# Query, key and value products of two chunks at a time by seven block products, with the query norm applied in the attention's sigmoid

## The chip, the cores and the metric

One core of a Trainium2 chip runs the whole program. The metric is device time in microseconds (us), the median of the runs shown. All arrays are float32. For TensorE the program keeps each operand as a pair of tiles of type float32r, a rounded high part and the rest (low part), and a product is three matmuls: high by high, low by high, high by low.

## What is computed

Two layers over 2048 tokens of 1024 channels. Layer A is a gated pooling mixer; layer B is causal stick-breaking attention with 16 heads of 64. What matters here, cut from the reference:

```python
kv_in = rms_norm(x, kv_norm)
k_all, v_all = jnp.split(kv_in @ w_kv, 2, axis=-1)
k_sh = rms_norm(split_heads(k_all), k_norm)
v_sh = split_heads(v_all)
h = rms_norm(x, b_norm[j])
q, z = jnp.split(h @ b_w_in[j], 2, axis=-1)
q = rms_norm(split_heads(q), b_q_norm[j])
o = stick_breaking_attention(q, k_sh, v_sh)   # beta = sigmoid(q.k / sqrt(d))
```

q, k and v are each a product of the stream (2048 x 1024) with a 1024 x 1024 matrix, whose rows carry the norm's gain.

## The kernel before

The first part of the program walks over four chunks of 512 tokens. For each chunk, layer A runs as 16 steps: eight of `run_z` and `run_u` (input projection), four of `run_o` (output projection), four of `run_g` (gated embedding), each 48 to 60 matmuls of 128x512. Then come six steps of `run_kvq` (L530 on): q, k, v, two column halves each. A step takes its weights as pairs from a list of loads made one step ahead (`load_w`: SP starts the transfer, ScalarE scales by the gain at L112, VectorE takes the rest at L113; without a gain ScalarE casts at L106 and POOL or VectorE subtracts at L108). In `run_kvq` two banks take 48 matmuls in turns, 24 each (L536), with the chunk's tokens as rows of the bank. ScalarE empties a bank with the token's norm as scale (L617 for q and k, L579 for v). For q and k follow a square (L619), a sum over each head (L621), the root on POOL (L80), a multiplication on VectorE (L629), four transposes (L638) and a split (L646, L647 or L215, L216), then a store of 512 KB to `qd` or `kd` (L649). Values are shifted by a token with transfers of ScalarE's queue, subtracted on POOL (L609), cast (L610) and split (L611), then stored.

Beside the steps run pieces of other work: `prep` turns the next chunk's x into pairs (L266, L269, L270) inside `run_kvq`, and `keep` (L700 on, its stores at L713) splits weights that the attention will read back, one or two a step from step 8 of a chunk on.

The second part is the attention over all heads and chunks, one slot for 128 queries by 512 keys: two matmuls (L816, L817), a sigmoid of the negative logits on ScalarE (L820), a scan on VectorE (L825, L828), transposes (L841), a cast and a rest (L844, L845), two matmuls with the values (L853, L854), with the remaining projections in the gaps.

The order on each engine is made by a scheduler from the order of the code, priorities and its own estimate of costs; each engine then works through its list in order and waits by semaphores. The banks of the first part are six (`psd` four, `psboth` two) for products and two (`pst`) for transposes. Pools: `io` 10 tiles for transfers (shared), `wraw` 3, `act` 18 pairs, `tmp` 8, `wpair` 6 and 6.

## Time and profile before

| what | value |
|---|---|
| runs | 2768.14, 2768.68, 2774.12 us; median 2768.68 |
| profiled execution, from the first to the last instruction | 2765.4 us; its time outside the span isn't given apart, and the median lies 3.3 us above the span |
| TensorE / VectorE / ScalarE / POOL busy | 2725.7 / 1956.0 / 1385.5 / 873.7 us |
| first part (layer A, q, k, v) | 0 to 1364.6 us |
| q, k, v stages of chunks 0 to 3 | 143.1, 143.0, 143.6, 139.2 us |
| attention | 1364.6 to 2765.4 us |
| moved by DMA | 573.21 MB, mean 207 GB/s |

An engine that is busy the whole span can only finish earlier by doing less; one with idle time costs nothing unless the busy one waits for it. So the rows to read are TensorE's waits and the busy time of every engine stage by stage. A group's row gives the line, engine, operation, tiles written and read, the count, then busy us and mean ns of one, then idle time just before and what ended it. PE is TensorE, DVE is VectorE, ACT is ScalarE, POOL is GpSimd.

### The profile page before, as it was taken

How to read it: one execution, taken by the hardware profiler on the slowest of the kernel's cores; microseconds unless marked ns; L12 is line 12 of the kernel's file. 1: busy time of each engine (PE TensorE's matmuls, PEld its weight loads, DVE VectorE, ACT ScalarE, POOL GpSimd, SP SyncE). 2: the span in 40 equal slices, each digit the busy share in tenths (PEclk: the TensorE clock that was granted, in tenths of full speed). 3: DMA queues.
4: the chain of work that ended last, by engine and by line, in shares of the span. 5: the costliest groups of instructions: out<-in, count | busy, mean ns of one | idle time of the engine just before them, and what ended most of it. 6: DMA issues, size and time to landing. Idle time of an engine off the chain costs nothing. (4 is left out here: it accounts for less than half of the span.)

```text
span 2765.4 us, 39537 instructions
## 1 busy us (share of the span) xinstructions
PE 2725.7 (99%) x13715; PEld 2260.4 (82%) x13715; DVE 1956.0 (71%) x2573; ACT 1385.5 (50%) x2801; POOL 873.7 (32%) x695
## 2 busy tenths in 40 slices
PE   9999999999999999999999999999999999999999
PEld 7888888888888888888888888887887778888877
DVE  6766535655357544565499999999999988996632
ACT  5444532445234542345356566666666655664521
POOL 2574338642475325753121111111110011112220
PEclk9999999999999999999999999999999999999999
DMA  8664696747946479445678565555555566668765
GB/s 293 236 196 171 218 325 204 225 148 253 347 148 227 163 249 318 136 145 170 191 254 278 180 217 170 169 161 178 169 159 162 159 200 200 188 204 264 249 209 160
DMA packets 335835, 573.21 MB, mean 207 GB/s; under 512 B 32462, under 2 KB 166638, under 8 KB 335636
## 3 DMA queue, kind: packets, MB, share of 16 engines
q1 hardware_dynamic: 330186, 563.03, 63.5%
q10 hardware_dynamic: 5450, 7.66, 0.9%
q8 instruction: 108, 1.77, 0.3%
q14 instruction: 91, 0.75, 0.1%
HBM read 430.01 MB, written 132.19 MB: 203 GB/s over the span
## 5 line engine op out<-in xcount | busy, mean ns | idle before, releaser
L844 ACT CAST at<-psa 128x512 fp32r<-128x512 f32 (+3 forms) x640 | 334.1, 522 | 478.4 <-PE psa L841 459.6
L536 PE MATMUL psd<-wpair,x 128*128 128x512 f32 x2304 | 544.0, 393 | 0.0
L828 DVE TENSOR_TENSOR_SCAN pp<-kap,pp,zeros 128x512 f32<-128x512 f32 x384 | 512.9, 1336 | 3.1 <-ACT kap L820 2.4
L536 PEld LDWEIGHTS psd<-wpair,x 128*128 128x128 f32 x2304 | 428.2, 188 | 86.2
L845 DVE TENSOR_TENSOR at<-psa,at 128x512 fp32r<-128x512 f32 (+3 forms) x640 | 381.0, 596 | 88.0 <-ACT at L844 84.9
L841 PE MATMUL psa<-ident,pp 128*128 128x128 f32 x2176 | 347.0, 275 | 17.2 <-DVE at L845 15.5
L820 ACT ACTIVATE kap<-psl 128x512 f32<-128x512 f32 (+3 forms) x640 | 344.9, 539 | 15.1 <-PE psl L817 12.0
L841 PEld LDWEIGHTS psa<-ident,pp 128*128 128x128 f32 x2176 | 262.9, 140 | 93.0 <-DVE at L845 38.8
L816 PE MATMUL psl<-kk,qa 128*128 128x512 f32 (+3 forms) x640 | 281.4, 440 | 0.0
L854 PE MATMUL pso<-at,vv 128*128 128x512 f32 (+3 forms) x640 | 235.1, 367 | 0.0
L817 PE MATMUL psl<-kk,qb 128*128 128x512 f32 (+3 forms) x640 | 233.0, 364 | 0.0
L853 PE MATMUL pso<-at,vv 128*128 128x512 f32 (+3 forms) x640 | 232.7, 364 | 0.0
L825 DVE TENSOR_TENSOR_SCAN pp<-kap,ahead 128x128 f32<-128x128 f32 (+3 forms) x256 | 219.8, 859 | 5.8 <-ACT kap L820 4.1
L131 PE MATMUL psd<-xp,wpair 128*128 128x512 f32 x512 | 201.9, 395 | 1.3 <-ACT xp L269 0.8
L132 PE MATMUL psd<-xp,wpair 128*128 128x512 f32 x512 | 200.5, 392 | 0.0
L133 PE MATMUL psd<-xp,wpair 128*128 128x512 f32 x512 | 200.1, 391 | 0.0
L113 DVE SCALAR_TENSOR_TENSOR wpair<-wraw,gains,wpair 128x512 fp32r<-128x512 f32 x192 | 169.7, 905 | 36.8 <-ACT wpair L112 36.1
L923 POOL TENSOR_TENSOR zr<-zr,sgz 128x512 f32<-128x512 f32 x32 | 58.8, 1836 | 368.2 <-ACT sgz L922 311.3
L112 ACT ACTIVATE wpair<-wraw,gains 128x512 fp32r<-128x512 f32 x192 | 135.0, 720 | 59.0 <-PE psd L536 32.3
L108 POOL TENSOR_TENSOR wpair<-wraw,wpair 128x512 fp32r<-128x512 f32 x99 | 145.5, 1485 | 59.7 <-ACT wpair L106 59.7
L853 PEld LDWEIGHTS pso<-at,vv 128*128 128x128 f32 x640 | 120.2, 188 | 26.9 <-ACT at L844 0.2
L854 PEld LDWEIGHTS pso<-at,vv 128*128 128x128 f32 x640 | 120.3, 188 | 25.9
(211 smaller groups left out, 5402.4 us busy)
## 6 DMA issues: line engine op xcount, KB each, us to landing
kk<-kd SPq DMA_DIRECT2D x320, 128.0 KB
vv<-vd SPq DMA_DIRECT2D x160, 256.0 KB
wraw<-in_w_kv_dram SPq DMA_DIRECT2D x128, 256.0 KB
wpair<-wzd SPq DMA_DIRECT2D x64, 512.0 KB
wpair<-wod SPq DMA_DIRECT2D x64, 512.0 KB
wpair<-wgd SPq DMA_DIRECT2D x64, 512.0 KB
wpair<-wu SPq DMA_DIRECT2D x48, 512.0 KB
wpair<-wi SPq DMA_DIRECT2D x36, 512.0 KB
```

What stands on the lines that cost most here:

```text
L131: T.matmul(ps, wst(units, kt, 0, c0), acts[kt][:, 0], start=(begin and kt == order[0]), stop=False)
L536: T.matmul(pss2[i], ck["x2"][kt][:, xh, tk], wst(ws, kt, wh, 0, W5), start=(kt == 0 and xh == 0 and wh == 0), stop=(kt == KT - 1 and wh == 1))
L816: T.matmul(ps[:, :w], qa[:, qs], kk[:, :w], start=True, stop=False)
L817: T.matmul(ps[:, :w], qb[:, qs], kk[:, :w], start=False, stop=True)
L820: A.activation(out=kp[:, r0:], in_=ps[:, :w], func=AF.Sigmoid, scale=-1.0)
L825: V.tensor_tensor_scan(out=pp[:, r0:][:, ::-1], data0=kp[:, r0:][:, ::-1], data1=ahead[:, r0:][:, ::-1], initial=1.0, op0=ALU.mult, op1=AL ...
L828: V.tensor_tensor_scan(out=pp[:, ::-1], data0=kp[:, ::-1], data1=zeros.to_broadcast([P, W5]), initial=st["carry"][j], op0=ALU.mult, op1=AL ...
L841: T.transpose(pt[:, j * P : (j + 1) * P], pp[:, r0 + kt * P : r0 + (kt + 1) * P], ident)
L844: A.copy(out=at[:, 0, cs], in_=pt[:, cs])
L845: V.tensor_tensor(out=at[:, 1, cs], in0=pt[:, cs], in1=f(at[:, 0, cs]), op=ALU.subtract)
L853: T.matmul(po[:, cs], vv[:, kt, :], at[:, 0, cs], start=(st["diag"] and kt == 0), stop=False)
L854: T.matmul(po[:, cs], vv[:, kt, :], at[:, 1, cs], start=False, stop=(st["last"] and kt == 3))
```

## The change

q, k and v are now computed for two chunks (e and e+1) together, after layer A of the odd one. For each kind the token rows are cut in two (the chunks) and the 1024 channels in two, so the stream is four blocks a11, a12 (chunk e) and a21, a22 (chunk e+1), and the weights b11, b12, b21, b22. In place of eight block products (512 tokens x 512 channels x 512 columns) there are seven, by Strassen's scheme in Winograd's form: with s1 = a21 + a22, s2 = s1 - a11, s3 = a11 - a21, s4 = a12 - s2, and sums of weight blocks likewise, the products are named "11", "21", 2, 1, "22", 3, 4. A step is one product of one kind (4 tiles of 128 tokens x 4 channel tiles x 3 = 48 matmuls). The order is products outside, kinds inside: "11" and "21" for k, q, v, then 2 for each, then 1 and "22", then 3 and 4, 21 steps for two chunks.

- Weight sums are made once, in steps 8 to 10 and 12 to 14 of layer A of chunks 0 and 1 (`combine`: 1 MB read, 1 MB written to DRAM a time), and read back for products 1 to 4; the splits of these need no gain. The weights kept for the attention move to chunks 2 and 3 and to the product steps.
- The stream's pairs (`x2p`) go to DRAM for all chunks and come back as left blocks; the sums are made from `x2d`, also read back (`sum12`, `sum4`, `sum3`).
- Product "11" is copied out by ScalarE, 2 and 1 are added to that by VectorE; "21", "22", 3, 4 add in the bank onto the product before and give the results (`final`), which mostly VectorE takes out of the banks with an addition. The second product of a step pair adds onto banks that the first has filled.
- q and k are no longer scaled by the token's norm; the norm's epsilon is scaled instead. The root of a query's head goes to a table, `qscale`, and the sigmoid takes its column as scale (the factor -1/sqrt(d) is in the gain). The keys keep their multiplication.
- Transposes wait by a clock of tiles and go in pairs of tiles; stores of heads are 256 KB with 1 KB rows.
- `prep` of the odd chunk runs inside `run_g` of the even one. Pools: `wraw` is gone, `act` 22, `tmp` 10; weights load two or three steps ahead. In the attention, `at` and the embedding pairs use `act`, and the last chunk's stream pairs are read back.

The core of the diff, with the new functions that make instructions:

```diff
+    def load_block(pools, src, base, gain, kind, block):
+        wpairs = pools
+        units = []
+        for k in range(4):
+            state["u"] += 1
+            pr = wpairs[state["u"] % 2].tile([P, 2, 1, W5], F32R, tag="wpair", name="wpair")
+            units.append(pr)
+            raw = io.tile([P, W5], F32, tag="io", name="wraw")
+            if block in (1, 2, 3, 4):
+                nc.sync.dma_start(out=raw, in_=wtd[kind, block, k])
+                A.copy(out=pr[:, 0, 0], in_=raw)
+                state["w"] += 1
+                on_pool = kind != "k" and state["w"] % 2
+                (G if on_pool else V).tensor_tensor(out=pr[:, 1, 0], in0=raw, in1=f(pr[:, 0, 0]),
+                                                           op=ALU.subtract)
+            else:
+                row, half = {"11": (0, 0), "21": (4, 0), "22": (4, 1)}[block]
+                col = base + (half ^ (kind == "v")) * W5
+                nc.sync.dma_start(out=raw, in_=src[(row + k) * P : (row + k + 1) * P, col : col + W5])
+                g = gain[:, row + k : row + k + 1]
+                A.activation(out=pr[:, 0, 0], in_=raw, func=AF.Identity, scale=g)
+                V.scalar_tensor_tensor(out=pr[:, 1, 0], in0=raw, scalar=g, in1=f(pr[:, 0, 0]),
+                                       op0=ALU.mult, op1=ALU.subtract)
...
+        def sum12(e, k):
+            a21, a22, a11 = fetch(e + 1, k), fetch(e + 1, 4 + k), fetch(e, k)
+            G.tensor_tensor(out=a22, in0=a21, in1=a22, op=ALU.add)
+            put(e, "s1", a22, V)
+            V.tensor_tensor(out=a11, in0=a22, in1=a11, op=ALU.subtract)
+            put(e, "s2", a11, G)
+        def sum4(e, k):
+            s2, a12 = couple[e // 2]["s2"][k], fetch(e, 4 + k)
+            G.tensor_tensor(out=a12, in0=a12, in1=f(s2[:, 0]), op=ALU.subtract)
+            V.tensor_tensor(out=a12, in0=a12, in1=f(s2[:, 1]), op=ALU.subtract)
+            put(e, "s4", a12, G)
+        def sum3(e, k):
+            a11, a21 = fetch(e, k), fetch(e + 1, k)
+            G.tensor_tensor(out=a11, in0=a11, in1=a21, op=ALU.subtract)
+            put(e, "s3", a11, V)
...
+        def run_block(e, kind, block, ws):
+            cp_ = couple[e // 2]
+            left = cp_[{"11": "a11", "21": "a12", 2: "s2", 1: "s1", "22": "s4", 3: "s3", 4: "a22"}[block]]
+            begin = block in ("11", 2, 1, 3)
+            banks, sums, nexts = (cp_[n].setdefault(kind, {}) for n in ("banks", "sums", "next"))
+            for i in range(4):
+                if begin:
+                    banks[i] = dense()
+                ps, tk = banks[i], slice(i * P, (i + 1) * P)
+                for k in range(4):
+                    for xh, wh in ((0, 0), (1, 0), (0, 1)):
+                        T.matmul(ps, left[k][:, xh, tk], ws[k][:, wh, 0, :],
+                                 start=(begin and k == 0 and xh == 0 and wh == 0),
+                                 stop=(k == 3 and wh == 1), skip_group_check=True)
+                if block in ("11", 1):
+                    if i % 2 == 0:
+                        cp_["pair", kind, block] = f(pair("sum"))
+                    (sums if block == "11" else nexts)[i] = cp_["pair", kind, block][:, i % 2]
+                first, second = int(kind == "v"), int(kind != "v")
+                if block == "11":
+                    A.copy(out=sums[i], in_=ps)
+                elif block == 2:
+                    V.tensor_tensor(out=sums[i], in0=ps, in1=sums[i], op=ALU.add)
+                elif block == 1:
+                    V.tensor_tensor(out=nexts[i], in0=ps, in1=sums[i], op=ALU.add)
+                elif block == "21":
+                    final(kind, e, first, i, ps, None)
+                elif block == "22":
+                    final(kind, e, second, i, ps, sums[i])
+                elif block == 3:
+                    final(kind, e + 1, second, i, ps, nexts[i])
                 else:
...
+                    final(kind, e + 1, first, i, ps, sums[i])
+                if kind != "k" and block in (3, 4) and i % 2 and "nxt" in chunk[e + 1]:
+                    next(chunk[e + 1]["nxt"], None)
+                tick()
...
+        def final(kind, s, b, j, ps, more):
+            t = out_tile(kind, s, b, j)
+            r2 = r2s[s][:, j : j + 1]
+            eps = epsall[:, s, j : j + 1]
             if kind == "v":
...
+                if more is None:
+                    A.activation(out=t, in_=ps, func=AF.Identity, scale=r2)
                 else:
...
+                    V.tensor_tensor(out=t, in0=ps, in1=more, op=ALU.add)
+                    A.activation(out=t, in_=t, func=AF.Identity, scale=r2)
+                later(1, lambda: values(s, b, j, t))
+                return
+            if more is None:
+                A.copy(out=t, in_=ps)
+            else:
+                V.tensor_tensor(out=t, in0=ps, in1=more, op=ALU.add)
+            keyed(s, kind, b, j, t, eps)
...
+            if kind == "q":
+                later(8, lambda: root(qscale[:, 4 * s + j, 8 * b : 8 * b + 8]))
+                turn_heads(s, kind, b, j, qs)
+                return
+            rq = t2.tile([P, 8], F32, tag="rq", name="rq", bufs=10)
+            root(rq)
+            def normed():
+                wide = rq.unsqueeze(2).to_broadcast([P, 8, HD])
+                tc.keep_in_program_order(V.tensor_tensor(out=qs, in0=qs, in1=wide, op=ALU.mult))
+                turn_heads(s, kind, b, j, qs)
+            later(6, normed)
...
-                nc.sync.dma_start(out=(kd if kind == "k" else qd)[s][4 * b + m], in_=f(hl))
-
-            for m in range(4):
-                lag.append(lambda m=m: finish(m))
+                dst = kd if kind == "k" else qd
+                for e in range(2):
+                    nc.sync.dma_start(out=dst[s][4 * b + m + e][:, :, (j - 1) * P : (j + 1) * P],
+                                      in_=f(hl)[:, :, e * 2 * P : (e + 1) * 2 * P])
...
-                for b in range(2):
-                    def load(wsrc=wsrc, base=base, b=b, gain=gain, s=s, kind=kind):
-                        return (load_w(wp, wsrc, KT, base + b * W5, W5, gain),)
-                    steps.append((load, lambda *w, s=s, kind=kind, b=b: run_kvq(s, kind, b, *w)))
+            if s % 2 == 0:
+                continue
+            for blocks in (("11", "21"), (2,), (1, "22"), (3, 4)):
+                for kind, wsrc, base, gain in (("k", w_kv, 0, g_kv), ("q", b_w_in[0], 0, g_b), ("v", w_kv, D, g_kv)):
+                    for block in blocks:
+                        def load(wsrc=wsrc, base=base, gain=gain, kind=kind, block=block):
+                            return (load_block(wp, wsrc, base, gain, kind, block),)
+                        steps.append((load, lambda *w, e=s - 1, kind=kind, block=block: run_block(e, kind, block, *w)))
...
+            t3, t2_ = tmp("ct3"), tmp("ct2")
+            G.tensor_tensor(out=t3, in0=b22, in1=b12, op=ALU.subtract)
+            G.tensor_tensor(out=b12, in0=b12, in1=b11, op=ALU.subtract)
+            V.tensor_tensor(out=t2_, in0=b22, in1=b12, op=ALU.subtract)
+            V.tensor_tensor(out=b21, in0=b21, in1=t2_, op=ALU.subtract)
+            for t, u in ((3, t3), (1, b12), (2, t2_), (4, b21)):
+                nc.sync.dma_start(out=wtd[kind, t, k], in_=u)
...
-            A.activation(out=kp[:, r0:], in_=ps[:, :w], func=AF.Sigmoid, scale=-1.0)
+            A.activation(out=kp[:, r0:], in_=ps[:, :w], func=AF.Sigmoid, scale=qscale[:, 4 * st["c"] + j, st["h"] : st["h"] + 1])```

**TensorE, in the q, k, v stage.** First before, in chunk 0 around the end of a step's first half (x_ are the stream's pairs by channel tile, qn the normalised heads, pst the banks for transposes):

```order
L536 MATMUL psd<-wpair,x_2497 128x512 x6
L536 MATMUL psd<-wpair,x_2502 128x512 x6
L536 MATMUL psd<-wpair,x_2637 128x512 x6
L536 MATMUL psd<-wpair,x_2642 128x512 x6
L638 MATMUL pst<-ident,qn 128x128 x8
L536 MATMUL psd<-wpair,x_2237 128x512 x6
L638 MATMUL pst<-ident,qn 128x128 x4
L536 MATMUL psd<-wpair,x_2242 128x512
L638 MATMUL pst<-ident,qn 128x128 x4
L536 MATMUL psd<-wpair,x_2242 128x512 x5
```

Now, at the end of product "21" of the queries and the start of "11" of the values (a_43 and a_44 are a12, a_40 and a_41 are a11):

```order
L651 MATMUL psd<-wpair,a_4426 128x512 x3
L651 MATMUL psd<-wpair,a_4428 128x512 x3
L781 MATMUL pst<-ident,qs 128x128 x4
L651 MATMUL psd<-wpair,a_4010 128x512 x3
L651 MATMUL psd<-wpair,a_4012 128x512 x3
L651 MATMUL psd<-wpair,a_4149 128x512 x3
L651 MATMUL psd<-wpair,a_4151 128x512 x3
L781 MATMUL pst<-ident,qs 128x128 x4
```

A bank was filled by 24 matmuls in turns with its neighbour, and is now filled by 12 in one go; the transposes stand between tiles.

**VectorE, in the same stage.** Before, in chunk 0 (ssq are sums over heads):

```order
L621 TENSOR_REDUCE ssq<-sqq 128x8
L113 SCALAR_TENSOR_TENSOR wpair<-wraw,gains,wpair 128x512 x2
L621 TENSOR_REDUCE ssq<-sqq 128x8
L629 TENSOR_TENSOR qn<-qs,rq 128x512
L113 SCALAR_TENSOR_TENSOR wpair<-wraw,gains,wpair 128x512
L629 TENSOR_TENSOR qn<-qs,rq 128x512
L113 SCALAR_TENSOR_TENSOR wpair<-wraw,gains,wpair 128x512 x4
```

Now, where product 2 begins (sum are results kept so far, xsum and s_ the sums of the stream, vv the value differences of product "21"):

```order
L630 TENSOR_TENSOR xsum<-xsum,s_4643 128x512
L662 TENSOR_TENSOR sum<-psd,sum 128x512
L630 TENSOR_TENSOR xsum<-xsum,s_4756 128x512
L662 TENSOR_TENSOR sum<-psd,sum 128x512 x2
L136 TENSOR_TENSOR wpair<-wraw,wpair 128x512 x2
L742 TENSOR_TENSOR vv<-vs,vv 128x8x64 x3
L662 TENSOR_TENSOR sum<-psd,sum 128x512
L630 TENSOR_TENSOR xsum<-xsum,s_4923 128x512
```

Before, no operation of VectorE here emptied a product's bank; now the additions from `psd` stand in line behind sums of the stream, which wait for POOL, and behind value differences, which wait for a transfer.

**SP, in layer A.** Before, during the gate steps of chunk 1 (kraw and kpair are the weights kept for the attention):

```order
L703 DMA kraw<-in_b_w_in_dram 128x4x128
L703 DMA kraw<-in_b_w_out_dram 128x4x128
L713 DMA wzd_291<-kpair 128x1024
L104 DMA wraw<-in_ple_gate_w_dram 128x2x256
L713 DMA wod_275<-kpair 128x1024
L104 DMA wraw<-in_ple_gate_w_dram 128x2x256
```

Now, in chunk 1 too (craw and ct are the weight blocks and their sums, wt_k the sums in DRAM):

```order
L864 DMA craw<-in_w_kv_dram 128x1024
L106 DMA wraw<-in_ple_gate_w_dram 128x2x256
L875 DMA wt_k_3_341<-ct_3662 128x512
L875 DMA wt_k_3_333<-craw 128x512
L875 DMA wt_k_3_337<-ct_3663 128x512
L875 DMA wt_k_3_345<-craw 128x512
L106 DMA wraw<-in_ple_gate_w_dram 128x2x256
```

The combinations' larger transfers stand between the gate's weight loads where the kept weights stood.

334 lines of the change are left out of this document (209 added, 125 removed).

## The prediction

> **What bounds the kernel now.** I read the page's totals and slices first, then TensorE's waits, then one table of stages.
>
> ```profile
> span 2765.4 us, 39537 instructions
> PE 2725.7 (99%) x13715; PEld 2260.4 (82%) x13715; DVE 1956.0 (71%) x2573; ACT 1385.5 (50%) x2801; POOL 873.7 (32%) x695
> PE   9999999999999999999999999999999999999999
> DVE  6766535655357544565499999999999988996632
> PEclk9999999999999999999999999999999999999999
> ```
>
> TensorE is busy 2725.7 of 2765.4 us, at full clock in every slice. Only 39.7 us of the span are not matrix work, so time can leave this kernel almost only with matmuls. VectorE is about half busy in the first half (projections) and nearly full in the second (attention). The list of what TensorE waited for is short:
>
> ```profile
> PE psa L841 <- DVE at L845: 15.5, 30, 1.6
> PE psao L986 <- DVE sg L980: 7.2, 4, 2.4
> PE pst L657 <- POOL ub L423: 2.3, 1, 2.3
> ```
>
> The first two belong to the attention. The table of stages, all engines (columns: stretch, its length, then busy us and count by engine, clock, DMA share, GB/s), cuts the span at the ends of layer A and of the q, k, v stage of each chunk:
>
> ```profile
> core 0: us, PE busy (x) PEld busy (x) DVE busy (x) ACT busy (x) POOL busy (x), PEclk, DMA share, GB/s
> 0.00:233.80 233.80, 226.59 (x1119) 188.72 (x1120) 159.65 (x268) 111.39 (x246) 120.44 (x105) 1.00 0.73 245
> 233.80:376.90 143.10, 143.06 (x681) 118.53 (x680) 74.11 (x109) 73.77 (x146) 48.53 (x44) 1.00 0.63 206
> 376.90:563.30 186.40, 186.40 (x830) 154.42 (x830) 103.80 (x122) 66.65 (x124) 122.72 (x99) 1.00 0.73 241
> 563.30:706.30 143.00, 142.96 (x681) 118.51 (x680) 71.77 (x110) 75.15 (x149) 49.05 (x44) 1.00 0.63 209
> ...
> 1225.40:1364.60 139.20, 139.16 (x649) 115.33 (x648) 65.73 (x95) 62.59 (x101) 44.32 (x40) 1.00 0.50 164
> 1364.60:1900.00 535.40, 527.84 (x2875) 436.90 (x2873) 506.90 (x607) 323.32 (x646) 79.13 (x46) 1.00 0.64 202
> 1900.00:2765.40 865.40, 842.51 (x4554) 700.90 (x4552) 690.08 (x919) 469.13 (x1008) 119.97 (x80) 1.00 0.63 193
> ```
>
> The stages that the change rewrites, 233.80:376.90 and its three successors, are TensorE end to end (143.06 of 143.10 us), with VectorE, ScalarE and the DMAs half used. A matmul less there is time less, one for one, until something else fills that stage.
>
> **What is removed.** Four chunks issue 2304 products on L536. Seven block products for eight leave 7/8 of them, 2016, as the built orders count too (all matmuls: 13701 before, 13413 after). So 288 go. The price of one is its spacing in an unbroken run:
>
> ```profile
> 245.53 16.81 PE L536 MATMUL psd<-wpair,x 128*128 128x512 f32 x73
> L536 PE MATMUL psd<-wpair,x 128*128 128x512 f32 x2304 | 544.0, 393 | 0.0
> 361.04 0.60 PE L266 MATMUL pst<-ident,xin 128*128 128x128 f32 x4
> 361.40 11.16 PE L536 MATMUL psd<-wpair,x 128*128 128x512 f32 x48
> ```
>
> The first row is 73 matmuls that span 16.81 us, the last of which takes 0.39: (16.81 - 0.39)/72 = 0.228 us. 288 x 0.228 = **65.7 us**. The group's busy time gives 544.0/2304 = 0.236 and 68.0 us, which counts the tails that lie beside transposes; I take the smaller. Transposes of heads stay 256 in number and those of x 128, so nothing else on TensorE changes size. A pair of chunks, 143.1 + 143.0 us, would take 286.1 - 32.8 - 2.8 = 250.5 us, where 2.8 is the eight groups of four x transposes (361.40 - 361.04 = 0.36 us each) that move into layer A of the even chunk, and are paid there.
>
> **VectorE in the new stage.** It gets the additions out of the banks, the sums of x, and more splits, and loses most weight scalings and the query normalisation. Rows for prices (busy us and mean ns of one, or min/median/max):
>
> ```profile
> L113 DVE SCALAR_TENSOR_TENSOR wpair<-wraw,gains,wpair 128x512 fp32r<-128x512 f32 x37 | 27.8, 773 | 6.0 <-ACT wpair L112 6.0
> L629 DVE TENSOR_TENSOR qn<-qs,rq 128x512 f32<-128x512 f32 x16 | 11.0, 690 | 11.8 <-POOL rq L80 11.7
> L108 DVE TENSOR_TENSOR wpair<-wraw,wpair 128x512 fp32r<-128x512 f32 x49 | 55.5, 1134 | 90.4 <-ACT wpair L106 79.3 <-POOL kpair L216 11.2
> L475 DVE TENSOR_TENSOR ta<-psd,ta x32: 671/676/684, 162.5 to 1171.9; 128x512 f32<-128x512 f32 x32
> L216 DVE TENSOR_TENSOR x<-tx,x x32: 677/1778/1796, 201.5 to 1228.7; 128x512 fp32r<-128x512 f32 x32
> L255 DVE TENSOR_TENSOR s2x<-parts x4: 167/168/169, 26.0 to 1039.5; 128x8 f32<-128x8 f32 x4
> ```
>
> Per pair of chunks: weight scalings 96 to 36, -60 x 0.773 = -46.4; plain weight splits +32 x 1.134 = +36.3; bank plus SBUF additions +60 x 0.676 = +40.6; query normalisations -16 x 0.690 = -11.0; small scalings +32 x 0.168 = +5.4; sixteen sums and splits of x, between 0.677 and 1.778 each, at 1.27 (the mean of that row's group) = +20.3. Together +45 on 74.11 + 71.77 = 145.9, so 191 of 250.5 us, 76%. POOL goes from 97.6 us by +16 weight splits and +20 sums at about 1.5, less 32 small operations at 0.4, and a few more of the weights kept for the attention, to some 145 us, 58%. ScalarE stays near its 149 us, since fewer weight casts pay for the copies out of the banks. Two stretches in which VectorE is that busy today and does empty banks are the gate parts of layer A:
>
> ```profile
> 376.90:468.00 91.10, 91.10 (x405) 75.45 (x405) 38.76 (x52) 24.22 (x46) 57.53 (x56) 1.00 0.83 282
> 512.00:563.30 51.30, 51.30 (x228) 42.46 (x228) 38.93 (x43) 28.31 (x51) 32.66 (x20) 1.00 0.74 246
> 842.00:894.30 52.30, 51.22 (x225) 41.78 (x224) 38.97 (x42) 27.39 (x51) 32.52 (x20) 1.00 0.73 243
> ```
>
> There VectorE is at 38.93/51.30 = 76% and TensorE idles 0, and 1.1 us the second time. In the attention's first stretch VectorE is at 95% and TensorE still loses only 535.40 - 527.84 = 7.6 us, 1.4%. For 2 x 250 us of new stage I bound the stalls by 0 and 2 x 1.1 x 250/52 = 10.6 us, both ends from rows, and take 1.4%: **+7**.
>
> **Transfers.** The new stage reads x sums and left blocks back from DRAM and stores head rows in 1 KB pieces. Per pair of chunks: today 206 and 209 GB/s over 143 us each are 59.4 MB. Weights fall by 12 blocks of 0.26 MB (-3.1), left blocks add 12 x 0.52 (+6.3), sums 24 x 0.26 (+6.3), kept weights for the attention about +4.4, x of the next chunk -2.1: 71 MB in 250 us, 285 GB/s. The row 376.90:468.00 carries 282 GB/s at a share of 0.83 with TensorE busy 91.10 of 91.10, so this is covered, with little to spare. The twelve combinations of weights (2.1 MB each, in the last half of layer A of chunks 0 and 1) take the place of kept weights there (0.8 MB a piece): +7 MB on about 110 us there, 65 GB/s on the 246 of the row 512.00:563.30, 310 at the worst. Bounds: 0, and what 28 GB/s above the covered 282 leave behind in three steps of 13 us, 1.1 MB or 4 us, in each of two chunks, so 8. I take **+2**, nearer to the covered row. POOL's and VectorE's share of a combination replaces that of the kept weights; SP issues each transfer in
>
> ```profile
> L104 SPq DMA_DIRECT2D wraw<-in_w_kv_dram x128: 327/376/1360, 217.2 to 1313.6; - x128
> ```
>
> 0.376 us, and some 256 issues per pair of chunks are 96 of 250 us: no bound.
>
> **The sigmoid.** Its scale becomes a column of numbers instead of a constant. Both kinds stand in the trace, from a bank to SBUF:
>
> ```profile
> L617 ACT ACTIVATE qs<-psd,r2all x64: 666/687/702, 247.3 to 1320.1; 128x512 f32<-128x512 f32 x64
> L820 ACT ACTIVATE kap<-psl 128x512 f32<-128x512 f32 x448 | 270.2, 603 | 11.8 <-PE psl L817 8.9
> ```
>
> +0.084 us on 640 is 54 us more of ScalarE, which is 60% busy in 1364.60:1900.00 (323.32 of 535.40) and 54% after. It is covered; TensorE names ScalarE in none of the waits above. Bounds 0 and 5 (a third of TensorE's 15.5 us behind VectorE, which waits for these), **+1** taken. The query row's 64 multiplications less on VectorE save nothing on the path.
>
> **Sum.** 2765.4 - 65.7 + 7 + 2 + 1 = 2709.7 for the profiled execution. The span is 3.3 us under the median of 2768.68, so the median should be **2713 us**.
>
> **Rivals.**
> (1) *A wait moves in front of the banks.* Today ScalarE empties q, k, v banks; then VectorE does, and its queue also holds the value differences, which wait for a transfer (rows of the order in the section on the change). Today:
>
> ```profile
> DVE vv L611 <- ACT vv L610: 19.2, 2, 11.3
> ```
>
> Two waits in a chunk, 19.2 us together and the longest 11.3, cost nothing now. In a step of two blocks a bank is written again three tiles later, 3 x 12 x 0.228 = 8.2 us. A wait of 11.3 then costs 3.1; two in each of four chunks are 25: 2738. If the slack is used up already, all 4 x 19.2 = 77 us count, and it is 2790. Against it: with six banks a step of one block has five tiles of slack, 13.7 us.
>
> (2) *Slower: VectorE becomes the bound, held off by POOL.* The row of x<-tx shows one operation at 0.677 or at 1.778, and an operation from a bank never above 0.684 (L475). Weight splits with two SBUF inputs average 0.773 where POOL is 34% busy (48.53 of 143.10). Per pair of chunks some 116 operations have two SBUF inputs (36 scalings, 32 splits, 16 normalisations, 16 sums, 16 value splits) and 132 one or a bank. At 1.778 and 0.68 that is 206 + 90 = 296 us against 250.5: 46 too many, twice, or 92, and 2713 - 10 + 92 = **2795**. It beats today only while the mean of the first kind stays under (250.5 + 32.8 - 90)/116 = 1.67; it begins to cost at 1.38. Against it: at POOL's estimated 58%, a good part of it small powers that read 8 elements a row, I expect 0.95 to 1.2, 200 to 229 us. The Trainium skill, "SBUF — State Buffer", section "Who interferes with whom", has this as a rule: a VectorE instruction with two SBUF inputs and a GpSimd one that reads SBUF exclude each other for the whole instruction, while one SBUF input does not contend. The trace agrees (1.778 against 0.684 us), and the rule speaks against this change.
>
> (3) *No change: the stage is bound by its transfers.* If 71 MB in smaller pieces run at 252 GB/s, the pair takes 283 us, as much as today, and the result is near 2768. For it: 246 GB/s is what the gate part moves; against it: 282 with room left.
>
> That the products don't fall away is excluded by the count.
>
> **Chances.** Forecast case (2700 to 2728): 0.66. Rival 1 (2728 to 2755): 0.16. Rival 3: 0.06. Rival 2 and the full form of rival 1 (over 2774): 0.12. The range 2700 to 2755 holds the first two. A measurement of this kernel tells about 0.2%, 5.5 us, from no change. Faster 0.82, same 0.06, slower 0.12.
>
> **What would show it.** Right: TensorE's busy time near 2660, its new products back to back, its waits for VectorE in the pair stages under some 7 us in sum, plain DVE additions from a bank at 0.68. Rival 1: TensorE waiting for the additions just where VectorE waits for value casts. Rival 2: VectorE over 95% in both pair stages, and splits at 1.4 us or more. Rival 3: DMA share near 1 and TensorE waiting for weights or left blocks. What would make me wrong otherwise: an idle TensorE at the start of a pair, whose left blocks and sums need the chunk just written.

## The result, and the profile after

The changed kernel takes **2863.28 us** (median of 4 runs, 2862.18 to 2865.78) against 2768.41 before: a ratio of 1.034, 95% interval 1.0325 to 1.0354. It is 95 us slower, where 55 us faster was forecast. The page of the changed kernel:

```profile
span 2860.8 us, 39730 instructions
PE 2713.5 (95%) x13427; PEld 2227.7 (78%) x13427; DVE 2063.7 (72%) x2725; ACT 1451.1 (51%) x2809; POOL 979.9 (34%) x731
PE   9988989998999999999889999999999999999999
DVE  6654466676455457666778989899999988996632
```

TensorE has 288 matmuls less, and its busy time falls by 12 us instead of 66. The reason stands in the view of the cores, first the changed kernel, then the one before:

```profile
core 0: 2860.8 us, clock 0.980
```

```profile
core 0: 2765.4 us, clock 0.999
```

A mean clock of 0.980 takes 2860.8 x 0.020 = 57 us off the span, but the clock is also low in part of the time in which TensorE stands still (0.68 from 187 to 197 us, where no matmul runs), and that costs nothing more. I laid the stretches at half clock of the trace over the matmul records: 42 us of them slow matmuls (0 before). At full clock TensorE would have been busy 2713.5 - 42 = 2671 us against 2725.7, 55 less. Idle time rose from 39.7 to 147.3 us. The balance is -55 + 108 + 42 = +95. By stages (columns as in the tables of the prediction; layer A of chunks 0 and 1, pair 0, layer A of chunks 2 and 3, pair 1, attention):

```profile
core 0: us, PE busy (x) PEld busy (x) DVE busy (x) ACT busy (x) POOL busy (x), PEclk, DMA share, GB/s
0.00:261.10 261.10, 235.72 (x1152) 195.06 (x1153) 159.10 (x258) 121.49 (x264) 124.41 (x108) 0.96 0.65 224
261.10:466.00 204.90, 193.06 (x838) 158.10 (x837) 114.17 (x121) 67.93 (x108) 131.46 (x105) 0.97 0.69 238
466.00:756.20 290.20, 262.99 (x1178) 212.75 (x1176) 189.46 (x290) 139.17 (x267) 142.95 (x100) 0.95 0.83 265
756.20:961.70 205.50, 194.29 (x862) 159.73 (x861) 104.33 (x130) 74.53 (x162) 119.93 (x101) 0.98 0.73 242
961.70:1150.50 188.80, 188.13 (x837) 155.03 (x836) 108.04 (x122) 64.91 (x118) 118.95 (x96) 1.00 0.64 214
1150.50:1424.50 274.00, 254.41 (x1147) 207.01 (x1145) 185.78 (x282) 130.02 (x237) 146.31 (x99) 0.97 0.83 262
1424.50:2860.80 1436.30, 1384.91 (x7423) 1140.03 (x7423) 1202.82 (x1526) 853.03 (x1655) 195.91 (x124) 0.99 0.64 195
```

Idle is the length less PE busy; the loss to the clock counts half of the time at half clock in which TensorE was busy (by the same count from the trace).

| stage | length before | after | idle after (before) | lost to the clock |
|---|---|---|---|---|
| layer A, chunk 0 | 233.8 | 261.1 | 25.4 (7.2) | 5.7 |
| layer A, chunk 1 | 186.4 | 204.9 | 11.8 (0) | 4.6 |
| pair 0 | 286.1 | 290.2 | 27.2 (0.1) | 12.0 |
| layer A, chunk 2 | 188.0 | 205.5 | 11.2 (1.1) | 3.6 |
| layer A, chunk 3 | 187.5 | 188.8 | 0.7 (0.6) | 0 |
| pair 1 | 282.9 | 274.0 | 19.6 (0.3) | 6.9 |
| attention | 1400.7 | 1436.3 | 51.4 (30.5) | 9.5 |

Without idle time and slowed clock the pairs would have taken 251 and 247.5 us, close to the 250.5 of the prediction. Only pair 1 got shorter. On TensorE, layer A of chunk 3 and the attention compute what they did before, layer A of chunk 2 only the moved transposes more, and these three together took 54 us longer. TensorE's waits, the longest in sum:

```profile
PE psa L1067 <- DVE at L1071: 30.2, 48, 2.9
PE pst L292 <- DVE ple L243: 17.6, 2, 10.6
PE psd L651 <- DVE sum L664: 9.9, 4, 3.3
PE psd L651 <- DVE qs L692: 9.3, 2, 6.0
PE psd L159 <- ACT x L242: 7.4, 2, 5.6
PE pst L781 <- DVE hl L243: 7.4, 5, 3.4
```

There is no single big wait. In the pairs alone, waits for product banks make 21.1 us (L664 and L692, emptied by VectorE, and 2.0 us for L660 of ScalarE), waits for transposition banks and heads 20.6 (L781, L292, also behind VectorE), left blocks and first query heads 5. The first three in pair 0:

```profile
PE pst L781 <- DVE hl L243: 5.9, 4, 3.4
PE psd L651 <- DVE sum L664: 5.0, 2, 2.9
PE pst L292 <- DVE hl L243: 3.4, 1, 3.4
```

One of them, the second, followed back by timelines (start, length, instruction, and in brackets the idle time before it): TensorE, VectorE and ScalarE of the changed kernel at the start of product 1 of pair 0.

```profile
583.25 11.14 PE L651 MATMUL psd<-wpair,s 128*128 128x512 f32 x48
597.30 23.45 PE L651 MATMUL psd<-wpair,s 128*128 128x512 f32 x96 [2.90 <-DVE sum L664]
```

```profile
592.48 1.55 DVE L887 SCALAR_TENSOR_TENSOR kpair<-kraw,gains,kpair 128x128 fp32r<-128x128 f32 x4 [1.82 <-ACT kpair L886]
593.95 0.68 DVE L662 TENSOR_TENSOR sum<-psd,sum 128x512 f32<-128x512 f32 x1
595.32 1.24 DVE L136 TENSOR_TENSOR wpair<-wraw,wpair 128x512 fp32r<-128x512 f32 x1 [0.69 <-ACT wpair L133]
596.48 0.68 DVE L664 TENSOR_TENSOR sum<-psd,sum 128x512 f32<-128x512 f32 x1
```

```profile
591.10 0.62 ACT L242 CAST kpair<-kraw 128x512 fp32r<-128x512 f32 x1 [2.81 <-DMA kraw<-in_ple_gate_w_dram]
592.04 1.28 ACT L886 ACTIVATE kpair<-kraw,gains 128x128 fp32r<-128x128 f32 x4 [0.32 <-DMA kraw<-in_b_w_in_dram]
594.04 0.62 ACT L133 CAST wpair<-wraw 128x512 fp32r<-128x512 f32 x1 [0.72 <-DMA wraw<-wt_q]
```

A bank is free when VectorE's addition (L662, L664, 0.68 us) has read it. In VectorE's list the rest of a kept weight (L887) and of a weight sum (L136) stand in front of the additions; each waits for ScalarE's cast; and ScalarE, in order too, waits for the transfers. VectorE is busy 65% of this stage, yet TensorE waits for it. The longest wait in the pairs (6.0 us before 1363.5, in pair 1, for L692) has value work in it as well: three value differences (L742, 2.5 us) stand in VectorE's list ahead of the addition, and ScalarE's casts of weights stand behind the starts of the value shifts.

What a stall does afterwards, in the same kernel: the stretch right behind this stall, and the next.

```profile
597.30:600.70 3.40, 3.40 (x9) 2.75 (x10) 0.63 (x2) 1.01 (x2) 1.91 (x3) 0.57 0.91 303
600.70:620.00 19.30, 19.30 (x87) 15.81 (x86) 12.01 (x21) 9.48 (x18) 9.94 (x8) 1.00 0.84 277
```

9 matmuls in 3.40 us where 15 are usual: the clock was granted at 0.57, and the stall of 2.90 us cost nearly half as much again.

### The profile page after: what moved, and what is told of

Read it like the earlier page. It is cut to its first block, busy times and chain, and to the rows that moved or that the text cites. A ratio compares the mean times of both kernels' runs of the same rounds, so it can differ in the third digit from the quotient of the medians.

```text
span 2860.8 us, 39730 instructions
## 1 busy us (share of the span) xinstructions
PE 2713.5 (95%) x13427; PEld 2227.7 (78%) x13427; DVE 2063.7 (72%) x2725; ACT 1451.1 (51%) x2809; POOL 979.9 (34%) x731
## 2 busy tenths in 40 slices
PE   9988989998999999999889999999999999999999
DVE  6654466676455457666778989899999988996632
## 5 line engine op out<-in xcount | busy, mean ns | idle before, releaser
L1071 DVE TENSOR_TENSOR at<-psa,at 128x512 fp32r<-128x512 f32 (+3 forms) x640 | 380.2, 595 | 99.6 <-ACT at L1070 96.5
L1046 ACT ACTIVATE kap<-psl,qscale 128x512 f32<-128x512 f32 (+3 forms) x640 | 401.3, 629 | 32.5 <-PE psl L1043 21.5
L1067 PE MATMUL psa<-ident,pp 128*128 128x128 f32 x2176 | 351.9, 277 | 32.2 <-DVE at L1071 30.2
L1067 PEld LDWEIGHTS psa<-ident,pp 128*128 128x128 f32 x2176 | 262.7, 141 | 115.1 <-DVE at L1071 63.9
L651 PE MATMUL psd<-wpair,s 128*128 128x512 f32 x1152 | 277.6, 400 | 9.9 <-DVE sum L664 9.9
L1042 PE MATMUL psl<-kk,qa 128*128 128x512 f32 (+3 forms) x640 | 282.2, 441 | 1.7 <-DMA qa<-qd 1.5
L651 PEld LDWEIGHTS psd<-wpair,s 128*128 128x128 f32 x1152 | 219.1, 192 | 56.9 <-issue 9.5
L1043 PE MATMUL psl<-kk,qb 128*128 128x512 f32 (+3 forms) x640 | 235.8, 369 | 0.0
L1051 DVE TENSOR_TENSOR_SCAN pp<-kap,ahead 128x128 f32<-128x128 f32 (+3 forms) x256 | 221.6, 868 | 11.5 <-ACT kap L1046 6.2
L651 PE MATMUL psd<-wpair,a 128*128 128x512 f32 x864 | 215.6, 406 | 14.8 <-DVE qs L692 9.3
L159 PE MATMUL psd<-xp,wpair 128*128 128x512 f32 x512 | 202.7, 397 | 5.3 <-DMA wpair<-wu 2.5
L651 PEld LDWEIGHTS psd<-wpair,a 128*128 128x128 f32 x864 | 166.2, 196 | 52.3 <-DVE qs L692 10.1
```

The source lines that it names most:

```text
L159: T.matmul(ps, wst(units, kt, 0, c0), acts[kt][:, 0], start=(begin and kt == order[0]), stop=False)
L651: T.matmul(ps, left[k][:, xh, tk], ws[k][:, wh, 0, :], start=(begin and k == 0 and xh == 0 and wh == 0), stop=(k == 3 and wh == 1), skip_g ...
L1042: T.matmul(ps[:, :w], qa[:, qs], kk[:, :w], start=True, stop=False)
L1043: T.matmul(ps[:, :w], qb[:, qs], kk[:, :w], start=False, stop=True)
L1046: A.activation(out=kp[:, r0:], in_=ps[:, :w], func=AF.Sigmoid, scale=qscale[:, 4 * st["c"] + j, st["h"] : st["h"] + 1])
L1051: V.tensor_tensor_scan(out=pp[:, r0:][:, ::-1], data0=kp[:, r0:][:, ::-1], data1=ahead[:, r0:][:, ::-1], initial=1.0, op0=ALU.mult, op1=AL ...
```

## The experiments

Each time is a median, from the same chip as runs of the kernel before, whose medians were 2767.0 to 2769.0. "After" is the changed kernel, to which each edit is made if nothing else is said.

**e5: only the matmuls less, in the kernel before.**

```diff
-                for kt in range(KT):
+                for kt in range(KT - 1):
                     for i in range(2):
...
```

> The kernel before, with the last eighth of the channels left out of the q, k and v products (288 matmuls less of L536, nothing added; that part of the products is not computed). Theory 'sum': TensorE was the bound there and 288 x 0.228 = 65.7 us go, 2768.5 - 65.7 = 2703. Theory 'hidden bound': if the stage cannot run in 125 us a chunk whatever is added, because of its transfers or VectorE, less than 50 us go, over 2718.

2722.4 us, ratio 0.9837 (0.9823 to 0.9852): 44.6 us less. The stage of chunk 0, from its first product to its last (143.2 us with 72 matmuls more in the kernel before), the first part, and its longest wait:

```profile
235.40:365.10 129.70, 127.26 (x610) 105.20 (x609) 71.22 (x107) 70.87 (x135) 47.33 (x43) 1.00 0.66 217
0.00:1318.60 1318.60, 1295.48 (x6004) 1069.88 (x6005) 759.02 (x1049) 591.52 (x1148) 672.95 (x571) 1.00 0.67 225
PE pst L638 <- DVE xp L270: 8.1, 8, 1.9
```

TensorE's busy time in the first part falls from 1355.4 to 1295.5, but its idle time rises from 9.3 to 23.1, and 7.8 of these 13.8 us are the wait shown for a transposition bank (0.3 before). The stage shrank by 13.5 of 16.4 us. By its number the result belongs to 'hidden bound' (over 2718), though the stage did get shorter: even with nothing added, a third of the 65.7 us doesn't come. That this is because all other work has an eighth less time is my reading; the runs don't show it apart.

**e2, e12, e13: the weight combinations.** e2 leaves them out, e12 keeps only their transfers, e13 only their loads and engine work.

```diff
-                nc.sync.dma_start(out=raw, in_=wtd[kind, block, k])
+                row, col = (block % 2) * 4, base + (block // 3) * W5
+                nc.sync.dma_start(out=raw, in_=src[(row + k) * P : (row + k + 1) * P, col : col + W5])
...
-            aside[i // 6, (8, 9, 10, 12, 13, 14)[i % 6]] = [combo]
+            pass
```

> The changed kernel without the twelve weight combinations in layer A of chunks 0 and 1; products 1 to 4 read plain weight blocks of the same size instead (the sums of weight blocks are left out). Theory 'combinations': their transfers and ScalarE's scalings, in order ahead of the gate's weights, make the waits in those two stages (25.4 and 11.8 us of idle TensorE against 7.2 and 0 before, plus 10 and 6 us of slowed clock); without them the stages come back to about 237 and 189 us, and the time is 2820 to 2830. Theory 'transposes': the x transposes that moved into the gate part want banks that its own transposes hold, whoever is late; then the idle stays near 10 us in chunk 0, chunk 2 keeps its 11, and the time is 2845 to 2863.

2824.8 us, 38.5 less. Layer A of chunks 0 and 1 is as it was before:

```profile
0.00:236.70 236.70, 230.01 (x1151) 192.34 (x1152) 142.19 (x251) 108.09 (x252) 109.34 (x100) 1.00 0.59 203
236.70:423.90 187.20, 187.20 (x837) 155.31 (x836) 99.24 (x110) 58.58 (x99) 110.22 (x89) 1.00 0.59 204
```

The moved transposes of x are still in chunk 0 here, with no loss: the combinations are the cause.

```diff
-                A.activation(out=raw, in_=raw, func=AF.Identity, scale=g)
...
-            G.tensor_tensor(out=t3, in0=b22, in1=b12, op=ALU.subtract)
-            G.tensor_tensor(out=b12, in0=b12, in1=b11, op=ALU.subtract)
-            V.tensor_tensor(out=t2_, in0=b22, in1=b12, op=ALU.subtract)
-            V.tensor_tensor(out=b21, in0=b21, in1=t2_, op=ALU.subtract)
-            for t, u in ((3, t3), (1, b12), (2, t2_), (4, b21)):
+            for t, u in ((3, b22), (1, b12), (2, b11), (4, b21)):
```

> The changed kernel with the weight combinations' transfers alone: rows are loaded and stored, the scaling and the four sums are left out. Theory 'engines': what delays chunk 0's and 1's layer A is ScalarE, VectorE and POOL work, each in order ahead of the gate's weights, and then nearly all of the 38 us come back, 2823 to 2833. Theory 'transfers': the combinations' 2 MB each and SP's in-order issue make the gate's weights late; then less than 12 come back, 2850 to 2863.

2824.9 us: all of the 38 come back. Chunk 0 then moves 310 GB/s and takes 10 us more than in e2; pair 0 is 6.5 us shorter than there, pair 1 and the attention are 3 to 4 us shorter each, which makes it good (why is not shown). Chunk 1 is undisturbed:

```profile
0.00:246.90 246.90, 233.64 (x1151) 194.79 (x1152) 140.66 (x251) 108.83 (x252) 108.07 (x100) 0.98 0.90 310
246.90:434.10 187.20, 187.20 (x837) 155.26 (x836) 99.22 (x109) 58.58 (x99) 110.22 (x89) 1.00 0.56 186
```

```diff
-            for t, u in ((3, t3), (1, b12), (2, t2_), (4, b21)):
-                nc.sync.dma_start(out=wtd[kind, t, k], in_=u)
```

(with the reads of plain blocks as in e2)

> The changed kernel with the combinations computed but not stored; products 1 to 4 read plain weight blocks (the results of the sums are left unused). Theory 'SP held by stores': 25 us or more of the 38 come back, 2823 to 2838. Theory 'engines': less than 12 come back, 2850 to 2863. Between them: the two share it.

2851.5 us: 11.7 come back. Chunks 0 and 1 are 12.6 and 11.1 us shorter than in the changed kernel (248.5 and 193.8), and later stages lose half of that again. So the engine work is the condition (without it, nothing is lost in sum), and more than half of its harm in these two stages goes with the stores. They stand in SP's queue until a sum is made (SP waits 10 us for them from 160 to 205 us of the changed kernel), with the gate's weights behind them; in sum, though, only 11.7 of the 38 us come back without them, and where the later stages lose the rest is not followed up.

**e3, e14, e6: the kept weights.** e3 makes 14 of 56, none in the pairs; e14 transfers all, but splits none (raw weights loaded twice); e6 starts the stores of kept and combined weights on POOL's queue.

```diff
-        for s in (1, 3):
-            places += [(s, 16 + i) for i in range(1, 13) for _ in range(2 - i % 2)]
+        for d in (wzd, wod, wgd, wld):
+            d[2:] = [d[o % 2] for o in range(2, KT)]
+        kept, places = kept[:14], [pl for pl in places if pl[1] != 8 and pl != (3, 14)][:14]
```

> The changed kernel with 14 of the 56 kept weight splits, all in layer A of chunks 2 and 3 and none in the pair stages; the attention reads the 14 again for the others (42 splits are left out). Theory 'queue': in the pair stages the stores of kept weights hold SP's queue (34 us of waits for POOL in each pair), so weights come late, ScalarE waits for them in order, VectorE's rests stand in front of the bank additions, and TensorE waits; without them the idle of the pair stages (27 and 18 us) and their slowed clock (14 and 8 us) fall by more than half, 2815 to 2835. Theory 'banks': the stalls come from the order of banks and additions itself (new product, same bank three tiles later), and stay; 2850 to 2863.

2838.5 us, 24.7 less. The two pairs:

```profile
465.30:741.20 275.90, 257.39 (x1178) 210.20 (x1177) 175.23 (x271) 126.15 (x234) 131.26 (x87) 0.97 0.73 232
1140.70:1398.10 257.40, 247.40 (x1146) 203.85 (x1145) 167.72 (x263) 118.25 (x204) 129.82 (x86) 0.99 0.72 229
```

Idle falls from 46.8 to 28.5 us in both together, and the waits for the sums (L664, L692) are gone.

```diff
-            raw = io.tile([P, kts, P], F32, tag="io", name="kraw")
...
+            for e in range(2):
+                nc.sync.dma_start(out=f(pr)[:, e], in_=src.rearrange("(k q) n -> q k n", q=P)[:, k0 : k0 + kts, o * P : (o + 1) * P])
```

> The changed kernel with the kept weights' transfers alone: the raw weights are loaded twice, as both halves of the pair, and stored, and the splits on ScalarE, POOL and VectorE are left out (0.26 MB more read for each piece than in the changed kernel). Theory 'engines and stores behind them': at least the 25 us that 42 pieces less gave come back, and chunk 2's 16 with them, 2815 to 2840. Theory 'transfers': nothing or a loss, 2855 to 2875.

2868.4 us: nothing comes back, though the splits are gone. The pairs, and layer A of chunk 2 between them:

```profile
468.20:755.70 287.50, 263.43 (x1178) 211.94 (x1176) 177.78 (x271) 126.00 (x234) 129.11 (x87) 0.95 0.89 282
755.70:969.80 214.10, 194.77 (x862) 159.95 (x861) 94.18 (x116) 68.06 (x143) 110.64 (x94) 0.96 0.93 301
1157.00:1430.20 273.20, 253.33 (x1146) 206.32 (x1144) 167.38 (x263) 116.88 (x204) 130.75 (x86) 0.98 0.84 267
```

So the transfers of the kept weights are enough to stall the pairs: with them at a DMA share of 0.84 and 0.89 the pairs idle 43.9 us, in e3 at 0.73 they idle 28.5. Whether the splits cost something as well stays open, since this run reads 0.26 MB more for each piece of 0.8 MB and carries 282 GB/s where the changed kernel carries 265.

```diff
-                nc.sync.dma_start(out=wtd[kind, t, k], in_=u)
+                nc.gpsimd.dma_start(out=wtd[kind, t, k], in_=u)
...
-            nc.sync.dma_start(out=dst, in_=f(pr))
+            nc.gpsimd.dma_start(out=dst, in_=f(pr))
```

> The changed kernel with the stores of kept and combined weights started from POOL's queue instead of SP's; nothing left out. Theory 'queue': SP's loads no longer stand behind stores that wait for POOL and VectorE, weights come in time, and the idle of chunk 0's and 1's layer A (25.4 and 11.8 us), chunk 2's (11.2) and of the pairs (27.2 and 19.6) falls by half or more with its slowed clock, 2800 to 2830. Theory 'work': it is ScalarE's and VectorE's added work and the DMAs' share that delay the banks; then little moves, 2850 to 2866.

2870.9 us, 7.6 more. Layer A of chunks 0 and 1 gains 6 us each, pair 0 loses 7. A store that waits takes its wait along: in pair 0 it is now POOL's list that waits for VectorE in front of such stores (9.7 us).

**e10: nearly no side work.** The edits of e2, and as in e3 only 14 kept splits, but all in chunk 3:

```diff
+        kept, places = kept[:14], [(3, i) for i in range(14)]
```

> The changed kernel without the weight combinations (products 1 to 4 read plain weight blocks) and with only 14 kept splits, all in layer A of chunk 3; both kinds of side work are left out elsewhere. If the two costs add (38.5 and 24.7 us by themselves) and chunk 2's 16 us of idle and slowed clock come from kept weights beside the moved x transposes, it is 2775 to 2790, and what is left over the sum of the prediction (2713) is the pairs' own stalls, about 35 us, and the attention's 35. If chunk 2's come from the transposes alone, 2793 to 2806.

2778.5 us, ratio 1.0035 (1.0022 to 1.0048). Chunks 0 and 1 are as in e2; then:

```profile
423.80:686.20 262.40, 252.48 (x1177) 207.24 (x1176) 169.44 (x266) 123.47 (x230) 125.58 (x86) 0.99 0.72 228
686.20:884.50 198.30, 193.07 (x863) 158.36 (x862) 98.20 (x120) 68.92 (x148) 112.68 (x95) 0.99 0.54 178
884.50:1086.50 202.00, 190.65 (x838) 157.19 (x837) 108.82 (x123) 65.51 (x120) 120.90 (x99) 0.97 0.73 247
1086.50:1342.70 256.20, 246.67 (x1147) 202.63 (x1145) 166.69 (x263) 117.94 (x204) 129.61 (x86) 1.00 0.73 229
```

Together the two give 84.8 us, more than the sum of each by itself (63.2). Chunk 2 recovers 7 of its 17 us, so kept weights beside the moved transposes were part of it. Chunk 3, with kept weights in 14 of its 16 steps, lost 13. Without this side work the pairs still have 19.5 us of idle time, and the kernel still isn't faster than before.

**e9 and e4: the same work at other places.** e9 puts the combinations in steps 0 to 11 of chunk 1 and most kept weights in layer A; e4 the transposes of x in later gate steps.

```diff
-            aside[i // 6, (8, 9, 10, 12, 13, 14)[i % 6]] = [combo]
+            aside[1, i] = [combo]
...
+        places = [(0, i) for i in (8, 9, 10, 11)] + [(1, i) for i in (12, 13, 14, 15)]
+        places += [(2, i) for i in (0, 1, 1, 2, 3, 3, 4, 5, 5, 6, 7, 7, 8, 9, 10, 11)]
...
```

> The changed kernel with all its side work, put at other places: the twelve weight combinations one a step in steps 0 to 11 of layer A of chunk 1 (none in chunk 0, none beside a gate step), the kept weights one or two a step in layer A, 4, 4, 16 and 22 in chunks 0 to 3, and 10 left in the pair stages in place of 36. Nothing left out. Theory 'place': the steps 0 to 7 of layer A read weights that need no split (ScalarE 10 to 40% busy there), so the side work delays no bank; chunk 0 loses its 28 us, chunk 1 most of its 18, chunk 2 most of its 16, the pairs some 20; 2780 to 2800. Theory 'amount': the same work costs the same wherever it stands, since transfers and VectorE share it; 2840 to 2866.

2871.8 us. Chunk 0 and pair 1 recover (242.2 and 260.7 us), chunk 1 grows to 227.6 and chunk 3 to 205.0, where TensorE now waits for the mixer's pairs:

```profile
PE psd L159 <- ACT mp L242: 10.7, 1, 10.7
```

At these places the same amount costs no less; that no place would be better is not shown.

```diff
-                    if kt in (3, 6) and s % 2 == 0:
+                    if kt in ((), (1, 4, 7), (1, 4, 7), (1, 4))[b] and s % 2 == 0:
```

> The changed kernel with the x transposes of the next chunk in the second to fourth gate steps only, three, three and two, instead of two in each of the four. Theory 'transposes': the 10.6 and 7.1 us waits for a transposition bank at the first gate step (chunks 0 and 2) and the slowed clock behind them go, 2835 to 2845. Theory 'combinations': the first gate step then waits for its weights or its embedding pairs instead, chunk 0 stays, and only chunk 2 gains, 2850 to 2860.

2860.6 us (2856.3 to 2865.2), which overlaps the changed kernel's own runs. Neither stage gets shorter (261.3 and 208.5 us): the waits move to a later gate step.

**e1, e7, e11, e15: the attention's 36 us.** e1 gives the sigmoid a constant (the query norm is not applied); e7 puts the scans' tiles in other memory; e11 ends the last pair with v, k, q; e15 is e11 without side work, as in e10.

```diff
-            A.activation(out=kp[:, r0:], in_=ps[:, :w], func=AF.Sigmoid, scale=qscale[:, 4 * st["c"] + j, st["h"] : st["h"] + 1])
+            A.activation(out=kp[:, r0:], in_=ps[:, :w], func=AF.Sigmoid, scale=1.0)
```

> The changed kernel with a constant as the sigmoid's scale in place of the table's column (the query norm's root is made, but not applied: that part of the computation is left out). The attention takes 1438 us in the changed kernel against 1401 before. Theory 'column': ScalarE's 0.09 us more on each of 640 sigmoids delays scan and transposes; then nearly all of the 37 us come back, about 2828. Theory 'start': the attention loses its time in its first 100 us, where it inherits the last pair's unfinished values and stores, and a slowed clock; then at most 10 us come back, 2853 to 2863, and the first 100 us still show about 14 us of idle TensorE.

2868.6 us (2863.5 to 2872.4): nothing. The sigmoid's own row, in the changed kernel and in e1:

```profile
L1046 ACT ACTIVATE kap<-psl,qscale 128x512 f32<-128x512 f32 (+3 forms) x640 | 401.3, 629 | 32.5 <-PE psl L1043 21.5
```

```profile
L1046 ACT ACTIVATE kap<-psl 128x512 f32<-128x512 f32 (+3 forms) x640 | 343.7, 538 | 39.6 <-PE psl L1043 30.9 <-DVE pp L1051 2.2 <-PE psl L1042 1.3
```

58 us more of ScalarE are wholly covered. Where the attention falls behind shows when the same points of its work are compared. From the first slot's logits to the 31st slot's, 311 or 312 matmuls, before and after:

```profile
1364.70:1425.30 60.60, 58.48 (x312) 48.15 (x311) 53.41 (x62) 33.68 (x67) 14.89 (x10) 1.00 0.73 218
```

```profile
1424.50:1504.90 80.40, 67.89 (x311) 51.73 (x311) 58.37 (x65) 37.06 (x68) 11.41 (x8) 0.92 0.69 199
```

That is 20 us. From the 61st to the 261st slot, before and after:

```profile
1483.50:1871.10 387.60, 385.81 (x2109) 321.05 (x2108) 369.33 (x442) 235.42 (x470) 55.40 (x31) 1.00 0.60 189
```

```profile
1562.00:1965.10 403.10, 391.24 (x2116) 319.99 (x2114) 373.03 (x444) 254.96 (x471) 55.92 (x31) 1.00 0.61 195
```

These are 15.5 more, of which 10 are new idle time. Outside the two stretches the attention nearly keeps its pace. The second loss stands, at 14 to 17 us, in the traces of all fourteen edits of the changed kernel: none touches it, and its cause stays open.

```diff
+        ppool = st.enter_context(tc.tile_pool(name="ppool", bufs=12))
         kap = st.enter_context(tc.tile_pool(name="kap", bufs=1))
-        ppool = st.enter_context(tc.tile_pool(name="ppool", bufs=12))
```

> The changed kernel with the scan's tiles of the attention in other memory: their pool is opened first, so that they lie where the first part had weight pairs and not where the last value differences wait for their stores (VectorE's first scan waits 4.5 us for such a store, and stands 9.7 us behind the first logits against 1.1 before). Nothing left out. Theory 'start': the attention's first 100 us lose 2 to 5 us instead of 14 and its slowed clock goes, 2838 to 2850. Theory 'bunched order': the scans stand six in a row in VectorE's list, the banks of the transposes still come late, and it is 2855 to 2866.

2859.6 us (2855.6 to 2862.6), 3.7 less. Now another tile waits for the same stores (VectorE's first instruction of the attention, 4.47 us), and the first scan still stands 10.9 us behind the first logits.

```diff
-                for kind, wsrc, base, gain in (("k", w_kv, 0, g_kv), ("q", b_w_in[0], 0, g_b), ("v", w_kv, D, g_kv)):
+                kinds = (("k", w_kv, 0, g_kv), ("q", b_w_in[0], 0, g_b), ("v", w_kv, D, g_kv))
+                for kind, wsrc, base, gain in (kinds if s < 3 or 3 not in blocks else (kinds[2],) + kinds[:2]):
```

> The changed kernel with the last two products of the last pair in the order v, k, q in place of k, q, v; nothing left out. Theory 'tail': the last value differences of both halves stand on VectorE, ScalarE and POOL when the attention starts, and its scan tiles wait for their stores; with the values 60 us... that is five steps of 12 us earlier, the first scan follows the first logits within 4 us (9.7 now), the first 100 us lose half of their 21 us of idle and slowed clock, 2838 to 2852, less what the late query heads make the first logits wait. Theory 'list': VectorE's list stays bunched, six scans in a row, whatever ends last; 2855 to 2866.

2861.8 us. The end of the last pair, and the attention:

```profile
1154.80:1444.40 289.60, 265.91 (x1194) 216.87 (x1192) 190.66 (x285) 131.82 (x239) 144.91 (x99) 0.96 0.84 264
1444.40:2858.70 1414.30, 1368.10 (x7376) 1127.97 (x7376) 1201.53 (x1524) 850.24 (x1652) 198.94 (x124) 1.00 0.63 194
```

The attention gets 22 us shorter and the pair 16 longer, but 47 matmuls have changed sides (x1147 and x7423 in the changed kernel): projections of the attention now run before its first logits, and 47 x 0.228 = 10.7 us are only counted elsewhere. What is left is 11 us gained in the attention and 5 lost in the pair, where the first logits wait 6.5 us for the last query heads.

> The changed kernel without side work (no combinations, 14 kept splits in chunk 3) and with the order v, k, q in the last pair's last two products. Without the order it took 2778.5. Theory 'tail': the attention comes to some 1415 us from 1435, and with weights in time the last heads don't make the end of the pair longer, 2758 to 2766, faster than the kernel before. Theory 'shifted': the end of the pair grows by as much as the attention shrinks, since some part of q, k or v always ends last, 2772 to 2780.

2770.6 us against e10's 2778.5: 8 less, ratio to before 1.0007 (0.9998 to 1.0017). The pair grew by 11.4 and the attention shrank by 16.7; 10.7 of both are the same 47 matmuls, so the pair hardly grew. The time lies between the two theories, and 'shifted' is not shown. The first stretch of the attention gains some 8 us of its 20, and the later 15 stay.

**e8: the value shifts started by POOL.**

```diff
-            queue = nc.sync if last else nc.scalar
+            queue = nc.sync if last else nc.gpsimd
```

> The changed kernel with the transfers that shift the values by a token started from POOL's queue instead of ScalarE's; nothing left out. ScalarE's casts and copies out of the banks stand behind these transfers in order (the 6.0 us wait of pair 1's last products follows 8 us of them). Theory 'ScalarE's queue': the waits for q's sums (6.0 and 3.2 us), their clock, and parts of the transposes' waits go, 2840 to 2852. Theory 'not there': the shifts cost no more than 4 us on the path, or POOL takes longer to start them; 2856 to 2880.

2873.3 us, 10 more. POOL is busy 170.9 us of pair 0 instead of 143.0, and VectorE 204.6 instead of 189.5.

## Why the prediction was wrong, point by point

- **The bound.** Right: TensorE's matrix work, its stalls and its clock make up the whole difference (-55 + 108 + 42).
- **-65.7 us.** Right where it was computed: without stalls and slowed clock the pairs take 498.5 us, forecast 501. Over the whole kernel only 55 us of matrix work at full clock are gone, since the other stages take 16 us more, 5.6 of them for the moved transposes. And the step "a matmul less there is time less, one for one" failed even by itself: in e5 65.7 us of matmuls gave 45.
- **VectorE, "stalls +7".** The step that failed. The busy times were right (VectorE 189 and 186 us, forecast 191; POOL 143 and 146, forecast 145), and the reading of them wrong. Stretches at 76% and at 95% that lost almost nothing were taken as the price of a stage at 76%. The pairs ran at 65% and 68% and lost 46.8 us to stalls and 19 to the clock, where 7 were forecast. What counts is not the share but what stands in the list ahead of the addition or the split that frees a bank, and on whose transfer that waits. Without the side work the idle time is 19.5 us (e10); what causes these stays open.
- **Transfers, "+2".** Failed twice. The rates were near (265 x 0.290 = 76.9 MB in pair 0, forecast 71 at 285 GB/s). But "covered" was read from a stretch with other waits; here most of the kept weights cost 25 us (e3), and their transfers alone are enough to stall the pairs (e14). And the combinations cost 38 us (e2) not by their transfers, the only thing that was priced (alone they cost 10 us in chunk 0 and nothing in all, e12), but by engine work, and by stores that wait for it in SP's queue (e13). The price of an edit that issues on four in-order lists was taken from one.
- **The moved transposes.** Costed at 2.8 us of TensorE. In chunk 0 that is right (e2); in chunk 2, beside kept weights, the stage lost 17.5, and without them still 10 (e10).
- **The sigmoid, "+1".** Right (e1). The "64 multiplications less" beside it are 32 (L629 ran 64 times, for queries and keys; L767 runs 32 times); nothing was added up from them.
- **The clock.** Not in the sum at all: 42 us of the 95.
- **The attention.** Not in the sum but for the sigmoid: 36 us. The caution named an idle TensorE at the start of a pair, which was 5 us in pair 0; the attention's loss was 20 us in its first 80, behind the end of the last pair, and 15 more between 140 and 540 us. The first part changes with the order of the last steps (e11, e15); how much a better order would save, and what the second part comes from, stays open.
- **Rivals.** The first had the mechanism, with only part of the culprits: waits did move in front of the banks, but in the wait followed back behind the rests of weights; value differences stand in the longest one, beside such rests. It was priced at 25 to 77 us in the pairs, and 66 came; but the chance of 0.16 was for its small form, and the full form shared 0.12 with the second rival. The second fell: splits from two SBUF inputs took 0.92 us in the mean where 1.67 would have been needed. The third gave the pairs' length (283 us; 290 and 274 came) and was right in one part, the kept weights' transfers, but the DMA share was 0.83 and not near 1.

No version found beats the kernel before: e15, without the combinations and three quarters of the kept splits, which the result needs, equals it.

## What to carry to other kernels

Price a stall in a stage by the list in front of the instruction that frees the bank, not by the engine's busy share, and give each piece of side work a price on every in-order list that it joins, the queue of its stores among them. Count a stall of TensorE of over some 2.3 us with the slowed clock behind it. Where an engine works while the clock is low, and where it only stands, are two things: only the first is a loss. Compare two kernels at the same points of their work, not at the same time or at a cut that matmuls can cross. An arithmetic saving of an eighth shortens the time in which all other work was hidden by an eighth as well: ask first what the stage before was hiding.

## What the runs showed of the hardware

The clock falls to half after surprisingly short stalls. In the granted clock of the traces of all these runs, I took the stalls of TensorE with no other of over 0.4 us within 8 us, without the program's first and last. Many are one stall seen in several runs. Of 151 between 0.75 and 1.75 us, 2 were followed by a stretch at half clock; of 49 up to 2.25 us, 11; of 38 up to 3 us, 34; of 71 longer ones, 70. Such a stretch lasts 3.4 us or a multiple. Counted while TensorE was busy, a stall of 2.25 to 3 us lost another 1.6 us in the mean, and one of over 6 us 2.4; of a long stall, part of the slowed stretch falls into the stall itself. The Trainium skill, "TensorE: Matmul & The Clock Gate", section "HAM oscillation — how this bites in real kernels", advises against gaps of over about 3.4 us; here most gaps over 2.25 us were enough.
